# A hybrid decoder step on one core: the down product of the ConvFFN computed as seven block products

## The chip, the cores and the metric

The kernel runs on one core of one Trainium2 chip. The metric is the device time of one execution, in microseconds. The core has five engines that run their own instruction queues in order: TensorE (PE, with its weight loads shown as PEld), VectorE (DVE), ScalarE (ACT), GpSimd (POOL) and SyncE (SP, which here only issues DMAs). They wait for one another by semaphores.

## The reference

One layer of a decoder for a prompt of 1024 tokens and 8 sequences of 8 new tokens, so 1088 columns in all. The part around the change is the gated ConvFFN and the last norm:

```python
    h = rms_norm(x, norm_ffn_g)
    g_full = jnp.concatenate([ffn_past, h @ w_ffn_gate], axis=1)
...
    x = x + (jax.nn.silu(g) * (h @ w_ffn_up)) @ w_ffn_down
...
    y_prompt = rms_norm(xp, norm_final_g)
    y_sample = rms_norm(xs, norm_final_g)
```

Here g is a causal convolution of width 3 over g_full. The model width D is 1024 and the FFN width is 2816. Ahead of it the layer has a convolution head group, a dilated attention with a cache, and an output product with a residual.

## The kernel before

Everything lies with channels on the 128 partitions and the 1088 columns (N) along the free axis. D is 8 tiles of 128 rows (KT), the FFN width 22 tiles, which are worked on in 11 **pairs** (j, j + 11). Each fp32 product is made of three matmuls in the fp32r format: a number is split into a rounded high part (hi, a copy on ACT) and a rest (lo, a subtraction, on DVE for activations and on POOL for weights), and hi·hi, hi·lo and lo·hi are summed in PSUM.

**The gate and up stage.** The normed activations h are cut in 2 by 2 blocks (upper and lower half of D, left and right half of the columns, HN = 544). In place of eight block products, seven are made from sums of blocks. The sums of h are made once and kept in SBUF under the tags b11, t2, b21, t1, t3, b22, t4, eight buffers [128, 544] each. The sums of the weights are made for every pair: `weight_raw` loads them (two raw buffers), `weight_parts` splits them (ACT L902, POOL L903), and `blocks_of_both` makes the sums on DVE (L918 to L921). `block_product` (L840, L842, L843) makes one of the seven: two column halves of 272, for each k three matmuls. Its results lie in `pair` tiles of PSUM (tag g2, four buffers of two banks). `ffn_pair(j)` makes the gate product, the convolution and silu, and the up product; the evictions of the up product are L1099 and L1103, the multiplication by silu(g) is `times` (L1094, L1096), and the two rows u of a pair go whole to DRAM (L1106, L1109), 544 KB each.

**The down stage** has pools of its own. The pairs are taken in groups (GROUPS: 3, 3, 3, 2). For a group, `load_act` reads the rows u (L1133) and splits them (hi on ACT L1135, lo on DVE L1136); `down` runs over the 8 output tiles m, loads and splits the weights (L143, L146, L148), and a plain product (L172 to L174, chunks of 384, 384 and 320 columns) is added to x2[m] (L1158), which was read back from DRAM (L1143). The acts of the next group are loaded in the midst of a group (`between`). The last group of two pairs is run by `last_product` in column chunks (TAIL) with m inside (L1195 to L1197); after each chunk but the first the final norm of the chunk before is made by `last_norm`: `rstd` sums the squares by matmul (L191), makes the root on DVE and ACT (L195 to L206), and spreads it by transposes on PE (L213). The sums of `rstd` have PSUM buffers of their own there (tag r, 2 buffers, beside 5 of tag g).

**Norm before the FFN.** `out_half` makes the output product by column halves; in the second half a hook, `norm_first`, issues the norm of the first half after tile m = 3.

The order of instructions on each engine is set by a scheduler that takes the program's order and its own model of times; a DMA or an instruction can be held behind another by `issue_after`.

Of the kernel before, what the change touches and what calls it, by code (L numbers as in the profile page):

```python
# [24 lines left out]
P = 128  # L25
# [18 lines left out]
GROUPS = ((0, 3), (3, 3), (6, 3), (9, 2))  # L44
TAIL = ((0, 256), (256, 256), (512, 320), (832, 256))
# [12 lines left out]
WR = 2  # L58
# [3 lines left out]
ACTS, XF = 22, 3  # L62
# [15 lines left out]
def trunk_kernel(tc, xT, w_in, w_out, w_gate, w_up, w_down, par, kc, vc, sa, sf, pmask, smask,  # L78
                 yT, kT, vT, ca, cas, cf):
    nc = tc.nc  # L80
    with (
# [817 lines left out]
        def weight_parts(x, new):  # L899
# [5 lines left out]
            return [(hi[:, i:i + 4], lo[:, i:i + 4]) for i in range(0, n // P, 4)]  # L905

        def blocks_of_first(raw):
            return weight_parts(raw[0], [zt("F", "WA", 2, "wa", D, F32R) for _ in range(2)])

        def blocks_of_both(raw):  # L910
            def wide(s):
                return wp.tile([P, D], F32R, tag="W", name=nm(s))

            g, u = raw
            t = wide("w22")
# [6 lines left out]
            s2, s4 = weight_parts(g, [wide("s24") for _ in range(2)])  # L922
            s3, s1 = weight_parts(u, [wide("s31") for _ in range(2)])
# [45 lines left out]
        def norm_first(m, added):  # L969
            if m == 3:  # L970
                r0.append(norm_half(sq0))
# [72 lines left out]
        ud = [dp.tile([P, N], F32, name=f"u{j}") for j in range(NF)]  # L1044
# [9 lines left out]
        def ffn_pair(j):  # L1054
# [46 lines left out]
            def put_u(i, h, ps, x):  # L1101
                o = u[i][:, h * HN:h * HN + HN]
                nc.vector.tensor_add(o, all_of(ps), o if x is None else x)  # L1103
# [12 lines left out]
        zf.__exit__(None, None, None)  # L1116


        zd = zones("D")
        zd.__enter__()  # L1120
        gbank[0], rbank[0] = ("D", "g", 5), ("D", "r", 2)

        def wide(s, dt=F32):
            return zt("D", "X", ACTS, s, N, dt)

        read = []

        def load_act(j0, n):
            act = []
            for i in range(2):  # L1130
                for j in range(j0 + i * HF, j0 + i * HF + n):
                    raw = keep("ur") if j0 == 0 else zt("D", "XR", XF, "ur")
                    read.append(nc.sync.dma_start(raw, ud[j]).ins)  # L1133
                    hi, lo = wide("ah", F32R), wide("al", F32R)
                    nc.scalar.activation(hi, raw, AF.Copy)  # L1135
                    nc.vector.tensor_sub(lo, raw, hi.bitcast(F32))  # L1136
                    act.append((hi, lo))
            return act

        def reload(m):  # L1140
# [180 lines left out]
```

## Time and profile before

| | |
|---|---|
| device time, median of 3 runs | 1427.86 us (1422.45 to 1429.79) |
| profiled execution, device time | 1432.72 us |
| profiled execution, span from first to last instruction | 1430.9 us |
| mean granted TensorE clock | 0.975 of full speed |
| gate and up stage, from first to last matmul of the pairs | about 652 to 1134.7 us of the span |
| down stage, groups 1 to 3 | 1134.7 to 1362.1 us |
| down stage, last group, and last norm | 1362.2 to 1430.9 us |

Times within the profile are microseconds from the start of the span. A row of a group gives busy time, the mean of one instruction and the idle time of the engine just before it, with what ended it. PEclk is the share of full clock granted to TensorE. Matmuls overlap, so the length of one is more than the distance from one to the next.

### The profile page before, as it was taken

The numbers are of one execution on the slowest core, as the hardware profiler recorded it, in microseconds if no ns is written. First come the engines' busy times: TensorE is split into PE (matmuls) and PEld (weight loads), VectorE is DVE, ScalarE is ACT, GpSimd is POOL, SyncE is SP. The second block draws the span as 40 slices with busy tenths as digits, with TensorE's granted clock in tenths as the row PEclk, the third lists the DMA queues.
The fourth block names the chain that finished last, engine by engine and source line by source line (L and its number), as shares of the span: only waits on it lengthen the run. The fifth ranks groups of instructions, "written<-read, shape, count | busy, mean of one in ns | idle before, by whom it ended". The sixth has DMA issues, their size and how long they took to land.

```text
span 1430.9 us, 24745 instructions
## 1 busy us (share of the span) xinstructions
PE 1350.0 (94%) x10011; PEld 1280.5 (89%) x10011; DVE 861.0 (60%) x1649; ACT 514.3 (36%) x982; POOL 431.5 (30%) x303
## 2 busy tenths in 40 slices
PE   6999999999999998976999999999999999999995
PEld 6988889999977777876899999999999889999995
DVE  7398595566574665679756566655656642423146
ACT  5312211457565564345333323333332321212033
POOL 3221111110000115231454445545445211224124
PEclk9999999999999998987999999999999999999998
DMA  7246676746699887340022122122212571414003
GB/s 271 54 139 245 226 255 206 206 141 179 180 276 226 243 228 225 112 162 8 30 91 91 65 87 91 52 70 91 91 62 91 167 291 45 139 48 131 11 9 118
DMA packets 84882, 195.16 MB, mean 136 GB/s; under 512 B 12576, under 2 KB 46752, under 8 KB 84768
## 3 DMA queue, kind: packets, MB, share of 16 engines
q1 hardware_dynamic: 84768, 193.57, 42.8%
q8 instruction: 79, 1.29, 0.4%
q14 instruction: 35, 0.29, 0.1%
HBM read 145.03 MB, written 48.52 MB: 135 GB/s over the span
## 4 chain that ended last, share of the span: by engine, by line
PE 76%; DVE 12%; DMA 6%; issue 2%; POOL 1%; ACT 1%; SPq 1%; POOLq 0%; ACTq 0%; DVEq 0%
PE g L174 9%; PE g L172 9%; PE g L173 9%; PE py L840 4%; PE py L842 4%; PE py L843 4%; DVE cacc L333 4%; PE o L666 3%; PE s L581 3%; PE pz L843 3%; PE pz L842 3%; PE pz L840 3%; PE px L843 3%; PE px L840 3%; PE px L842 3%; PE t L649 3%
## 5 line engine op out<-in xcount | busy, mean ns | idle before, releaser
L148 POOL TENSOR_TENSOR wl<-wr,wh 128x768 fp32r<-128x768 f32 (+2 forms) x61 | 117.1, 1921 | 464.7 <-PE g L174 391.8
L172 PE MATMUL g<-xh,wh 128*128 128x384 f32 (+1 forms) x472 | 158.6, 336 | 0.0
L173 PE MATMUL g<-xl,wh 128*128 128x384 f32 (+1 forms) x472 | 157.4, 333 | 0.0
L174 PE MATMUL g<-xh,wl 128*128 128x384 f32 (+1 forms) x472 | 157.2, 333 | 0.0
L172 PE MATMUL g<-ah,wh 128*128 128x384 f32 (+1 forms) x432 | 141.6, 333 | 5.0 <-ACT ah L1135 3.3
L173 PE MATMUL g<-al,wh 128*128 128x384 f32 (+1 forms) x432 | 143.0, 331 | 1.7 <-DVE al L1136 1.7
L174 PE MATMUL g<-ah,wl 128*128 128x384 f32 (+1 forms) x432 | 142.7, 331 | 0.7 <-POOL wl L148 0.7
L146 ACT ACTIVATE wh<-wr 128x768 fp32r<-128x768 f32 (+2 forms) x62 | 52.0, 838 | 241.0 <-PE g L174 177.5
L903 POOL TENSOR_TENSOR s<-wr,s 128x1024 fp32r<-128x1024 f32 x44 | 107.5, 2444 | 89.7 <-ACT s L902 47.9
L1158 DVE TENSOR_TENSOR x<-g,x 128x384 f32<-128x384 f32 (+1 forms) x72 | 38.0, 534 | 137.4 <-PE g L174 137.2
L622 ACT ACTIVATE y<-y,m 128x128 f32<-128x128 f32 (+1 forms) x192 | 88.4, 463 | 32.9 <-DVE m L610 32.9
L174 PEld LDWEIGHTS g<-xh,wl 128*128 128x128 f32 x472 | 90.0, 191 | 2.3 <-issue 2.1
L585 DVE CUSTOM_DVE_ANT_0 y<-s,pmk 128x128 f32<-128x128 f32 (+1 forms) x192 | 63.9, 378 | 45.8 <-PE s L581 36.9
L172 PEld LDWEIGHTS g<-xh,wh 128*128 128x128 f32 x472 | 90.1, 191 | 1.4 <-issue 1.2
L173 PEld LDWEIGHTS g<-xl,wh 128*128 128x128 f32 x472 | 90.0, 191 | 1.1 <-issue 1.0
L172 PEld LDWEIGHTS g<-ah,wh 128*128 128x128 f32 x432 | 82.0, 191 | 5.9 <-ACT ah L1135 3.6
L173 PEld LDWEIGHTS g<-al,wh 128*128 128x128 f32 x432 | 81.9, 190 | 2.0 <-DVE al L1136 2.0
L174 PEld LDWEIGHTS g<-ah,wl 128*128 128x128 f32 x432 | 81.8, 189 | 1.0 <-POOL wl L148 1.0
L333 DVE SCALAR_TENSOR_TENSOR cacc<-gp,prm,cacc 128x1024 f32<-128x1024 f32 x60 | 80.1, 1335 | 0.1
L1087 DVE SCALAR_TENSOR_TENSOR fc<-gb,prm,fc 128x1104 f32<-128x1104 f32 x44 | 79.0, 1813 | 2.0 <-ACT fc L1085 1.2
L903 POOL TENSOR_TENSOR wa<-wr,wa 128x1024 fp32r<-128x1024 f32 (+1 forms) x23 | 56.3, 2448 | 76.3 <-ACT wa L902 76.3
L381 DVE TENSOR_TENSOR qkv<-g,rb 128x384 f32<-128x384 f32 (+1 forms) x53 | 41.2, 777 | 46.0 <-PE g L174 45.9
(307 smaller groups left out, 4118.1 us busy)
## 6 DMA issues: line engine op xcount, KB each, us to landing
cr<-in_kc SPq DMA_DIRECT2D x24, 768.0 KB, 8.8
cr<-in_vc SPq DMA_DIRECT2D x24, 768.0 KB, 7.7
kk<-dk SPq DMA_DIRECT2D x48, 256.0 KB, 7.3
u<-u SPq DMA_DIRECT2D x22, 544.0 KB, 3.0
ur<-u SPq DMA_DIRECT2D x22, 544.0 KB, 4.8
wr<-in_w_in SPq DMA_DIRECT2D x22, 512.0 KB, 4.9
wr<-in_w_gate SPq DMA_DIRECT2D x22, 512.0 KB, 3.3
wr<-in_w_up SPq DMA_DIRECT2D x22, 512.0 KB, 4.5
```

Source lines behind the costliest of these rows:

```text
L148: lo_eng.tensor_sub(lo, raw, hi.bitcast(F32))
L172: nc.tensor.matmul(ps[c], whi[:, k, :], xh[:, t0:t0 + n], start=(k == 0), stop=False)
L173: nc.tensor.matmul(ps[c], whi[:, k, :], xl[:, t0:t0 + n], start=False, stop=False)
L174: nc.tensor.matmul(ps[c], wlo[:, k, :], xh[:, t0:t0 + n], start=False, stop=(k == nk - 1))
L333: eng.scalar_tensor_tensor(acc[:, :S], gp[:, j:j + S], col(w0 + j), acc[:, :S], op0=ALU.mult, op1=ALU.add)
L585: nc.vector.tensor_tensor_reduce(out=y[:, o:o + n], in0=ps[:, o:o + n], in1=mask, op0=ALU.add, op1=ALU.min, scale=1.0, scalar=3e38, accum_ ...
L622: nc.scalar.activation(y, y, AF.Exp, bias=m[:, 4 * g + i:4 * g + i + 1], scale=-1.0, accum_out=den[:, g, 2 * hd + u, i:i + 1])
L840: nc.tensor.matmul(ps, whi[:, k, :], xh[:, t], start=(start and k == 0), stop=False, skip_group_check=True)
L842: nc.tensor.matmul(ps, whi[:, k, :], xl[:, t], start=False, stop=False, skip_group_check=True)
L843: nc.tensor.matmul(ps, wlo[:, k, :], xh[:, t], start=False, stop=(k == nk - 1), skip_group_check=True)
L903: nc.gpsimd.tensor_sub(lo, x, hi.bitcast(F32))
L1087: nc.vector.scalar_tensor_tensor(c[:, :W], gb[i][:, t:t + W], col(C_FW + 3 * f + t), c[:, :W], op0=ALU.mult, op1=ALU.add)
```

## The change

Nine of the eleven pairs (three groups of three) of the down product are now made by the same seven block products. The two halves of the contraction are rows j and j + 11, the two halves of the output are tiles m and m + 4, and the two halves of the columns are as before. So a group has four units (m, m + 4), a unit seven block products of 18 matmuls with 272 columns, 12 units in all.

The block sums of u are made in `ffn_pair` for the nine pairs, by four subtractions of [128, 544] on DVE (L1124 to L1130), and stored as seven blocks of 272 KB in place of two rows of 544 KB. `load_block` reads a block back into the slot for its low part, makes the high part from it on ACT (L1148) and subtracts on DVE (L1149), 21 blocks for a group. They lie in the slots of the block sums of h, six of eight buffers; the other two hold accumulators: a unit has three results beside its four output blocks (`extra`, e1, e6, e7), which are added in with five additions in the last group (L1204). Evictions are L1179 (DVE) and, for the first group's extra results, L1183 (ACT). The weights of a unit go through `weight_parts` and `blocks_of_both` like those of the FFN.

One pool serves both stages. The last two pairs are made as before by `last_product`, now in four chunks of 272 columns, with acts and weights in slots of the shared pool. `rstd` takes its PSUM from the same four `pair` buffers as the products. The norm of the first half (`norm_first`) is issued after m = 5 in place of m = 3.

```diff
@@ -41,8 +41,9 @@
 BIG = 1e30
 LN2 = float(np.log(2.0))
 CHUNKS = ((0, 384), (384, 384), (768, 320))
-GROUPS = ((0, 3), (3, 3), (6, 3), (9, 2))
-TAIL = ((0, 256), (256, 256), (512, 320), (832, 256))
+GROUPS = ((0, 3), (3, 3), (6, 3))
+LAST = 9
+TAIL = ((0, 272), (272, 272), (544, 272), (816, 272))
...
@@ -896,22 +896,25 @@
                     nc.sync.dma_start(raw[-1], w[i])
             return raw
 
-        def weight_parts(x, new):
+        def weight_parts(x, new, parts=1):
             n = x.shape[-1]
             hi, lo = new
             nc.scalar.activation(hi, x, AF.Copy)
             nc.gpsimd.tensor_sub(lo, x, hi.bitcast(F32))
             hi, lo = [t.rearrange("p (k c) -> p k c", c=P) for t in (hi, lo)]
-            return [(hi[:, i:i + 4], lo[:, i:i + 4]) for i in range(0, n // P, 4)]
+            k = n // P // parts
+            return [(hi[:, i * k:i * k + k], lo[:, i * k:i * k + k]) for i in range(parts)]
...
@@ -967,7 +970,7 @@
         r0 = []
 
         def norm_first(m, added):
-            if m == 3:
+            if m == 5:
                 r0.append(norm_half(sq0))
 
@@ -1041,7 +1044,9 @@
             block_product(z, a22, blocks["t4"], False)
             put(1, 0, z, None)
 
-        ud = [dp.tile([P, N], F32, name=f"u{j}") for j in range(NF)]
+
+        ud = {j: dp.tile([P, N], F32, name=f"u{j}") for i in range(LAST, HF) for j in (i, i + HF)}
+        bd = [{tag: dp.tile([P, HN], F32, name=f"u{tag}{j}") for tag in BTAGS} for j in range(LAST)]
         M = S - HN
         W = GW - 2
 
@@ -1103,98 +1108,153 @@
                 nc.vector.tensor_add(o, all_of(ps), o if x is None else x)
                 if (i, h) == (0, 1):
                     times(0, HN, N)
-                    nc.sync.dma_start(ud[j], u[0])
                 elif x is None:
                     times(1, 0, N)
-                    nc.sync.dma_start(ud[j + HF], u[1])
+                else:
+                    return
+                if j >= LAST:
+                    nc.sync.dma_start(ud[j + i * HF], u[i])
+                    return
+                (x11, x12), (x21, x22) = halves(u[0]), halves(u[1])
+                if i == 0:
+                    nc.sync.dma_start(bd[j]["b11"], x11)
+                    return
+                nc.sync.dma_start(bd[j]["b21"], x21)
+                nc.sync.dma_start(bd[j]["b22"], x22)
+                nc.vector.tensor_sub(x11, x12, x11)
+                nc.sync.dma_start(bd[j]["t1"], x11)
+                nc.vector.tensor_sub(x12, x22, x12)
+                nc.sync.dma_start(bd[j]["t3"], x12)
+                nc.vector.tensor_sub(x22, x22, x11)
+                nc.sync.dma_start(bd[j]["t2"], x22)
+                nc.vector.tensor_sub(x21, x21, x22)
+                nc.sync.dma_start(bd[j]["t4"], x21)
 
             products(weight_blocks(w_up, j) if j else first_up_a + blocks_of_both(first_up), u11, put_u)
 
         for j in range(HF):
             ffn_pair(j)
         nc.sync.dma_start(cf, cfo.rearrange("p j c -> p (j c)"))
...
+
+
+
+        loads = []
+
+        def load_block(tag, j):
+
+            hi, lo = slot(tag, "uh"), slot(tag, "ul")
+            raw = lo.bitcast(F32)
+            loads.append(nc.sync.dma_start(raw, bd[j][tag]).ins)
+            nc.scalar.activation(hi, raw, AF.Copy)
+            nc.vector.tensor_sub(lo, raw, hi.bitcast(F32))
+            return hi, lo
 
         def rows(m, j0, n):
 
             return w_down[m].rearrange("p (i c) -> p i c", i=2)[:, :, j0 * P:(j0 + n) * P]
 
...
+        def down_raw(m, j0, n):
+            raw = []
+            for i in (m, m + 4):
+                t = wp.tile([P, D], F32, tag="WR", name=nm("wr"), bufs=WR)[:, :2 * n * P]
+                nc.sync.dma_start(t.rearrange("p (i c) -> p i c", i=2), rows(i, j0, n))
+                raw.append(t)
+            return raw
+
+        extra = {}
+
+        def down_unit(m, j0, n, ub, first, last):
+            raw = down_raw(m, j0, n)
+            a11, a12, a22, s1, s2, s3, s4 = blocks_of_first(raw) + blocks_of_both(raw)
+            if first:
+                for i in (m, m + 4):
+                    x2[i] = (keep if i in (0, 4, 1, 5, 2) else spare)("x2")
+                    with tc.issue_after(loads[3 * n - 1]):
+                        nc.sync.dma_start(x2[i], x2d[i])
+                extra[m] = [slot(BTAGS[1 + (3 * m + i) // 2], "ex", F32) for i in range(3)]
+            e1, e6, e7 = extra[m]
+            (c11, c12), (c21, c22) = halves(x2[m]), halves(x2[m + 4])
+
+            def add(o, ps):
+                nc.vector.tensor_add(o, all_of(ps), o)
+
+            def put(o, ps):
                 if first:
-                    reload(m)
-
...
+                    nc.scalar.activation(o, all_of(ps), AF.Copy)
+                else:
+                    add(o, ps)
+
+            x, y, z = pair("px"), pair("py"), pair("pz")
+            block_product(x, a11, ub["b11"], True)
+            put(e1, x)
+            block_product(y, s2, ub["t2"], True)
+            put(e6, y)
+            block_product(x, a12, ub["b21"], False)
+            add(c11, x)
+            block_product(y, s1, ub["t1"], False)
+            add(c22, y)
+            block_product(z, s3, ub["t3"], True)
+            put(e7, z)
+            block_product(y, s4, ub["b22"], False)
+            add(c12, y)
+            block_product(z, a22, ub["t4"], False)
+            add(c21, z)
+            if last:
+                for o, e in ((c12, e1), (e6, e1), (e7, e1), (c21, e6), (c22, e7)):
+                    nc.vector.tensor_add(o, o, e)
+
+        for q, (j0, n) in enumerate(GROUPS):
+            ub = {tag: [load_block(tag, j) for j in range(j0, j0 + n)] for tag in BTAGS}
+            for m in range(4):
+                down_unit(m, j0, n, ub, q == 0, q == len(GROUPS) - 1)
+
+
+        nl = HF - LAST
+        act = []
+        for i, j in enumerate(j for j0 in (LAST, LAST + HF) for j in range(j0, j0 + nl)):
+            tag = ("b11", "b11", "t2", "b21")[i]
+            act.append([])
+            for h in range(2):
+                hi, lo = slot(tag, "ah"), slot(tag, "al")
+                raw = lo.bitcast(F32)
+                nc.sync.dma_start(raw, ud[j][:, h * HN:h * HN + HN])
+                nc.scalar.activation(hi, raw, AF.Copy)
+                nc.vector.tensor_sub(lo, raw, hi.bitcast(F32))
+                act[-1].append((hi, lo))
+        nj = len(act)
         w = []
-
...
+        for m in range(KT):
+            if m % 2 == 0:
                 raw = wp.tile([P, D], F32, tag="WR", name=nm("wr"), bufs=WR)
...
+            r = raw[:, m % 2 * 512:m % 2 * 512 + 512]
+            nc.sync.dma_start(r.rearrange("p (i c) -> p i c", i=2), rows(m, LAST, nl))
+            if m < 2:
+                t = zt("F", "WA", 2, "wl", D, F32R)
+            elif m < KT - 1:
+                t = wp.tile([P, D], F32R, tag="W", name=nm("wl"))
+            if m < KT - 1:
+                hi, lo = t[:, :512], t[:, 512:]
+            else:
+                hi, lo = slot("t2", "wh", w=512), slot("t2", "wl", w=512)
+            nc.scalar.activation(hi, r, AF.Copy)
+            nc.gpsimd.tensor_sub(lo, r, hi.bitcast(F32))
+            w.append([t.rearrange("p (k c) -> p k c", c=P) for t in (hi, lo)])
+
+
+        def wide(s):
+            return slot(("t1", "t3", "b22", "t4")[cnt[0] % 4], s, F32)
 
         def last_product(t0, n):
             acc = [None, None]
+            h, t = divmod(t0, HN)
             for m in range(KT):
-                ps = bank(*gbank[0])
+                ps = pair()
...
-        zd.__exit__(None, None, None)
+        zf.__exit__(None, None, None)
         zr.__exit__(None, None, None)
```

Three places show how the instructions now stand. Numbers behind an underscore tell tiles of one name apart.

The first is ScalarE at the turn from one group of pairs to the next. Before, the last copies of the second group's acts (ah) and the weights (wh) of the tiles m:

```order
L146 ACTIVATE wh_12605<-wr_12603 128x768
L146 ACTIVATE wh_12671<-wr_12669 128x768
L1135 ACTIVATE ah_12191<-ur_12189 128x1088
L1135 ACTIVATE ah_12737<-ur_12735 128x1088
L146 ACTIVATE wh_12773<-wr_12771 128x768
L1135 ACTIVATE ah_12743<-ur_12741 128x1088
```

Now, with uh the high part of a block of u for the second group and s_1878 the high part of the weight sum for the first unit of that group (product with t2):

```order
L1148 ACTIVATE uh_12954<-ul_12955 128x544
L1148 ACTIVATE uh_12964<-ul_12965 128x544
L1148 ACTIVATE uh_12959<-ul_12960 128x544
L1148 ACTIVATE uh_12969<-ul_12970 128x544
L1148 ACTIVATE uh_12974<-ul_12975 128x544
L902 ACTIVATE s_1878_12994<-wr_12979 128x768
L902 ACTIVATE s_1880_12998<-wr_12981 128x768
L902 ACTIVATE wa_13142<-wr_13138 128x768
```

The weight parts stood between the acts, ahead of part of them; now the sums of the unit's weights stand behind the last block of the group (uh_12964, uh_12969 and uh_12974 are the blocks with tag t4). TensorE takes the products of that unit in this order, where px is the product with b21 and py_13003 the one with t2:

```order
L840 MATMUL px_13002<-uh_12914,wa_12983 128x272
L842 MATMUL px_13002<-ul_12915,wa_12983 128x272
L843 MATMUL px_13002<-uh_12914,wa_12984 128x272
L840 MATMUL py_13003<-uh_12889,s_1878_12994 128x272
L842 MATMUL py_13003<-ul_12890,s_1878_12994 128x272
L840 MATMUL pz_13004<-uh_12934,s_1880_12998 128x272
L842 MATMUL pz_13004<-ul_12935,s_1880_12998 128x272
L843 MATMUL py_13003<-uh_12889,s_1879_12995 128x272
```

The eighteen matmuls with b21 stand between the last product of the old group (with the old t4) and the first that reads s_1878.

The second place is TensorE in the last product, at the first norm of a chunk. Before, the sums (L191) and, 34 rows later, the transposes (L213):

```order
L1197 MATMUL g_13999<-ah_13319,wl_13348 128x256
L191 MATMUL r_14017<-ones,sq_13761 128x1 x2
L1195 MATMUL g_14055<-ah_13301,wh_13326 128x320
L1196 MATMUL g_14055<-al_13302,wh_13326 128x320
```

```order
L1197 MATMUL g_14087<-ah_13313,wl_13334 128x320
L213 MATMUL r_14031<-ident,rr_14023 128x128 x2
L1195 MATMUL g_14087<-ah_13319,wh_13333 128x320
```

Now:

```order
L1257 MATMUL g_14705<-ah_14406,wl_14450 128x272
L191 MATMUL g_2072_14723<-ones,sq_14467 128x1 x2
L191 MATMUL g_2072_14723<-ones,sq_14467 16x1
L213 MATMUL g_2077_14739<-ident,rr_14731 128x128 x2
L213 MATMUL g_2077_14739<-ident,rr_14731 128x16
L1255 MATMUL g_14764<-ah_14381,wl_14418 128x272
```

Matmuls of the next chunk stood between the sums and the transposes; now nothing does. The same holds for the second norm (42 rows between before, none now). For the third nothing stood between in either kernel.

The third place is VectorE at the end of a pair in the gate and up stage; u are the two rows of the pair, gb is the next pair's gate product, py and pz its results in PSUM. Before:

```order
L1103 TENSOR_TENSOR u_9151<-py_9204,ta_9201 128x544
L1094 TENSOR_TENSOR u_9151<-u_9151,fc_9139 128x480
L1096 TENSOR_TENSOR u_9151<-u_9151,fc_9139 128x64
L1103 TENSOR_TENSOR u_9152<-pz_9205,u_9152 128x544
L1094 TENSOR_TENSOR u_9152<-u_9152,fc_9146 128x1024
L1073 TENSOR_TENSOR gb_9363<-py_9419,ta_9416 128x544
```

Now:

```order
L1108 TENSOR_TENSOR u_10122<-py_10175,ta_10172 128x544
L1099 TENSOR_TENSOR u_10122<-u_10122,fc_10110 128x480
L1101 TENSOR_TENSOR u_10122<-u_10122,fc_10110 128x64
L1124 TENSOR_TENSOR u_10122<-u_10122 128x544
L1108 TENSOR_TENSOR u_10123<-pz_10176,u_10123 128x544
L1099 TENSOR_TENSOR u_10123<-u_10123,fc_10117 128x1024
L1126 TENSOR_TENSOR u_10122<-u_10123,u_10122 128x544
L1128 TENSOR_TENSOR u_10123<-u_10123,u_10122 128x544
L1078 TENSOR_TENSOR gb_10343<-py_10399,ta_10396 128x544
L1130 TENSOR_TENSOR u_10123<-u_10123 128x544
```

Three of the four subtractions stand ahead of the eviction of the next gate product (L1073 before, L1078 now); the fourth follows it.

More of the change, by code (lines that the diff above doesn't have):

```diff
@@ L1115, in trunk_kernel @@
         nc.sync.dma_start(cf, cfo.rearrange("p j c -> p (j c)"))
[L1116 to L1138, printed above, removed]
@@ L1145, in rows @@
         def rows(m, j0, n):
             return w_down[m].rearrange("p (i c) -> p i c", i=2)[:, :, j0 * P:(j0 + n) * P]
-        def down(j0, n, act, first, between):
-            for m in range(KT):
-                if m == 2:
-                    between()
-                w = load_w(rows(m, j0, n), 2 * n, nc.gpsimd)
-                if first:
-                    reload(m)
-                def ev(ps, t0, n, x=x2[m]):
-                    nc.vector.tensor_add(x[:, t0:t0 + n], ps[:, :n], x[:, t0:t0 + n])
-                gemm(w, act, 2 * n, ev)
+        def down_raw(m, j0, n):
[5 more added lines that the diff above has]
+            return raw
```

44 lines of the change are left out of this document (11 added, 33 removed).

## The prediction

> **What bounds the kernel now.** I read the page's busy table and the chain of waits first, then tables by stage, then PE's gaps.
>
> ```profile
> PE 1350.0 (94%) x10011; PEld 1280.5 (89%) x10011; DVE 861.0 (60%) x1649; ACT 514.3 (36%) x982; POOL 431.5 (30%) x303
> PE 76%; DVE 12%; DMA 6%; issue 2%; POOL 1%; ACT 1%; SPq 1%; POOLq 0%; ACTq 0%; DVEq 0%
> ```
>
> TensorE is busy for 94% of the span and holds 76% of the chain that ends last. So a microsecond of matmuls saved counts in full, and a gap on PE costs in full, as long as PE has no other gap to lose it in. Busy time by stage (columns: window, length, then busy and count for PE, PEld, DVE, ACT, POOL; PEclk; DMA share; GB/s):
>
> ```profile
> 800.00:900.00 100.00, 100.00 (x802) 100.00 (x801) 60.51 (x68) 30.32 (x34) 49.15 (x38) 1.00 0.26 87
> 1310.00:1362.00 52.00, 52.00 (x314) 52.00 (x313) 9.16 (x17) 3.40 (x4) 8.89 (x5) 1.00 0.11 31
> 1134.70:1362.40 227.70, 220.27 (x1300) 218.80 (x1299) 73.94 (x96) 44.87 (x47) 52.53 (x27) 0.99 0.35 117
> ```
>
> The gate and up stage and the end of group 3 run without a gap: 100/802 = 0.1247 us for a matmul of 272 columns, and 52/314 = 0.1656 us for the down product's mix (mean 362.7 columns). Per column that is 0.458 and 0.457 ns: a matmul has next to no fixed cost here, and columns are what counts. The whole of groups 1 to 3 takes 227.7 us for 1296 matmuls, which at full pace are 1296 x 0.1656 = 214.6 us: 13.1 us are lost. PE's gaps there:
>
> ```profile
> 1135.86 0.76 PE L172 MATMUL g<-ah,wh 128*128 128x320 f32 x3 [0.60 <-DVE u L1103]
> 1138.32 0.45 PE L173 MATMUL g<-al,wh 128*128 128x384 f32 x1 [1.70 <-DVE al L1136]
> 1151.25 1.91 PE L172 MATMUL g<-ah,wh 128*128 128x384 f32 x5 [3.29 <-ACT ah L1135]
> 1307.18 0.44 PE L172 MATMUL g<-ah,wh 128*128 128x384 f32 x1 [1.15 <-ACT wh L146]
> 1309.14 0.44 PE L174 MATMUL g<-ah,wl 128*128 128x384 f32 x1 [0.70 <-POOL wl L148]
> ```
>
> They sum to 7.4 us. The third brings a second loss, seen in windows of 2 us; the first row stands for comparison:
>
> ```profile
> 1138.00:1140.00 2.00, 1.68 (x10) 1.68 (x11) 2.00 (x3) 0.00 (x0) 0.00 (x0) 1.00 0.96 345
> ...
> 1150.00:1152.00 2.00, 0.75 (x2) 0.75 (x3) 0.77 (x1) 1.69 (x2) 0.00 (x0) 0.65 1.01 418
> 1152.00:1154.00 2.00, 2.00 (x8) 2.00 (x8) 1.96 (x3) 2.00 (x3) 0.00 (x0) 0.50 1.02 420
> 1156.00:1158.00 2.00, 2.00 (x9) 2.00 (x9) 0.26 (x1) 0.00 (x0) 0.00 (x0) 0.64 1.03 422
> ```
>
> After an idle time of 3.29 us the granted clock is 0.50 until about 1157.4 (0.64 over the last window), 6.2 us of work at half pace: 3.1 us lost. I call this the **clock penalty** and charge it to gaps of 3 us or more. After the gap of 1.70 us (first row) the clock stayed at full. The last 2.6 us of the 13.1 are spread in pieces too small to name.
>
> **Part 1, the matmuls.** 1296 matmuls of 362.7 columns become 12 x 126 = 1512 of 272: 1512 x 0.1247 = 188.5 us in place of 214.6: **-26.1**. All the losses of the old stage go with its code: **-13.1**. What the new stage loses in their place follows.
>
> **Part 2, entry into the down product.** The first unit needs 21 blocks (5.7 MB) in the slots that hold the block sums of h. A slot comes free when the last FFN product with its tag ends, for t4 at the very end; and DVE has the last pair's products and 21 low parts to make.
>
> ```profile
> ur<-u SPq DMA_DIRECT2D x22, 544.0 KB, 4.8
> 1135.84 1.22 DVE L1094 TENSOR_TENSOR u<-u,fc 128x1024 f32<-128x1024 f32 x1
> L883 DVE TENSOR_TENSOR t4l<-x,t4h 128x544 fp32r<-128x544 f32 x4 | 2.7, 716 | 0.0
> ```
>
> 21 x 0.72 = 15 us of low parts and, as I count its rows, about as much again of evictions, products and weight sums stand against the unit's 7 x 18 x 0.1247 = 15.7 us and the 18 us of the six FFN products (24 matmuls each) that follow when the first slots come free. VectorE has no slack there, but six tags of seven can be loaded ahead, which the old stage, with six rows of 4.8 us each to load and x2 to read back, could not; so it should be no worse than the old entry (0.60 + 1.70 + 3.29 + 3.1 = 8.7). Bounds 4 (two short waits) and 14 (a longer one and the penalty); I take **+8**, next to the old entry.
>
> **Part 3, the two turns between groups.** A group fills the slots, so a block can be loaded only after the old group's last product with it. On ACT the weight sums of the new unit (s_1878) stand behind all 21 block copies, the last three of which have the tag t4. PE gets to s_1878 only 18 matmuls, 2.2 us, after the old t4 product. From that product's end: load, copies, the high part of the sum; its low part on POOL is needed by the third matmul.
>
> ```profile
> x2d<-x SPq DMA_DIRECT2D x16, 272.0 KB, 2.0
> mx<-mixed SPq DMA_DIRECT2D x4, 272.0 KB, 4.6
> L882 ACT ACTIVATE t4h<-x 128x544 fp32r<-128x544 f32 x4 | 2.6, 657 | 1.3 <-DVE x L1000 1.2
> L146 ACT ACTIVATE wh<-wr 128x768 fp32r<-128x768 f32 x24 | 20.3, 847 | 125.3 <-PE g L174 104.9 <-DMA wr<-in_w_down 9.4 <-PE py L842 6.2
> L148 POOL TENSOR_TENSOR wl<-wr,wh 128x768 fp32r<-128x768 f32 x24 | 46.6, 1943 | 160.0 <-PE g L174 144.8 <-ACT wh L146 15.2
> L1103 DVE TENSOR_TENSOR u<-pz,u 128x544 f32<-128x544 f32 x11 | 7.8, 712 | 0.4 <-PE pz L843 0.4
> ```
>
> Lower end: 2.0 (a 272 KB store, the faster row) + 2 x 0.66 + 0.85 + 1.94 = 6.1, minus the 2.5 us that PE has work = 3.6 us of idle PE. With the load row of the same size: 4.6 + 3 x 0.66 + 0.85 + 1.94 - 2.5 = 6.9. VectorE gives a second chain: it has 17 low parts and 5 evictions ahead of the last weight sum, 22 x 0.72 = 15.8 us from about 6 us after the old b11 product ended; the old t4 product ends 15.7 us after that, so the sum is ready 6.1 + 0.6 later, and 6.7 + 0.85 + 1.94 - 2.5 = 7.0, or 10 where POOL's work slows four or five of the low parts to twice their time. Two chains meet at **7**, which I take. The clock penalty follows: 7 + 3 = 10 a turn (bounds 3.6 and 13), two turns **+20**. What is late next is the product with s_1880, whose parts follow on ACT and POOL by 0.85 and 1.94 us, within a product at half pace (4.5 us): nothing more.
>
> The Trainium skill (page "TensorE: Matmul & The Clock Gate", Part 1) puts the drop at an idle window of about 3.4 us and the recovery at about 3.4 us of sustained work. The drop agrees with the row at 1151.25; the recovery took 6.2 us there, so the row decides. By the page's figure an estimate of the penalty would be 1.7 us and the sum some 4 us lower.
>
> **Part 4, inside the units.** A unit has seven evictions (7 x 0.72) and four weight sums, 7 to 8 us of DVE in 15.7: covered. In the last group five additions of about 0.7 us each come on top and stand before the next unit's sums; the last product's acts and weights wait for slots too. Bounds 0 and 8, **+4**.
>
> **Part 5, the sums of u in the gate and up stage.** Four subtractions more for each of nine pairs. Where they fall:
>
> ```profile
> 882.51 2.41 DVE L1094 TENSOR_TENSOR u<-u,fc 128x480 f32<-128x480 f32 x1
> 885.72 2.68 DVE L1094 TENSOR_TENSOR u<-u,fc 128x1024 f32<-128x1024 f32 x1
> 890.45 0.72 DVE L1073 TENSOR_TENSOR gb<-py,ta 128x544 f32<-128x544 f32 x1 [2.05 <-PE py L843]
> 884.87 2.45 POOL L903 TENSOR_TENSOR s<-wr,s 128x1024 fp32r<-128x1024 f32 x1 [0.47 <-PE pz L843]
> 893.56 0.29 PE L840 MATMUL py<-t1h,s 128*128 128x272 f32 x1
> ```
>
> Before the eviction at 890.45 DVE idles 2.05 us, and PE needs it at 893.56, after 891.17: 2.4 us more. Three subtractions stand ahead of it: 2.2 us at 0.72, up to 4.3 where POOL's subtraction doubles them as it doubled the 1.22 us product to 2.68; one waits for a store of its operand (2.0 us or more). So 0 to 1.1 us a pair; nine pairs, bounds 0 and 10, **+5**. The gaps are too short for a clock penalty. The stores grow from 2 x 544 to 7 x 272 KB a pair, at a DMA share of 0.26 in that window: hidden behind products of 21 us a pass.
>
> **Part 6, norms.** In the last product the transposes now follow the sums at once.
>
> ```profile
> 1385.29 0.50 PE L191 MATMUL r<-ones,sq 128*128 128x1 f32 x4
> 1390.57 0.38 PE L213 MATMUL r<-ident,rr 128*128 128x128 f32 x2
> 1385.83 0.16 DVE L195 TENSOR_SCALAR rv<-r 128x2 f32<-128x2 f32 x1
> 1388.58 0.16 DVE L206 SCALAR_TENSOR_TENSOR rr<-rt,rr 128x2 f32<-128x2 f32 x1
> 1400.63 0.15 DVE L195 TENSOR_SCALAR rv<-r 128x2 f32<-128x2 f32 x1
> 1402.72 0.15 DVE L206 SCALAR_TENSOR_TENSOR rr<-rt,rr 128x2 f32<-128x2 f32 x1
> ```
>
> The roots took from 1385.3 to 1388.7 and from about 1400.3 to 1402.9, covered by matmuls. Without cover PE idles 3.3 and 2.4 us, and the first, as long as the one at 1151, brings a penalty of 3; the second may: bounds 5 and 11, **+9**. The earlier norm shows the same form:
>
> ```profile
> 626.25 1.18 PE L191 MATMUL g<-ones,sq 128*128 128x1 f32 x10 [1.73 <-DVE sq L955]
> 633.24 1.33 PE L213 MATMUL g<-ident,rr 128*128 128x128 f32 x5 [5.81 <-DVE rv L193]
> ```
>
> Two tiles later the first wait (1.73) should vanish, while the 5.81 and its penalty stay, with less work behind it: -3 to +2, **-0.5**. Four equal chunks end with 272 columns in place of 256: about 0, at most +-1.
>
> **The sum.** -26.1 - 13.1 + 8 + 20 + 4 + 5 + 9 - 0.5 = +6.3 us, from the profiled execution's 1432.7 (span 1430.9) to 1439. That execution lies 4.9 above the median of the three runs, 1427.9; the forecast on that scale is **1434**. The saved columns count in full, and the waits at the turns and the norms take them back.
>
> **Rivals.**
> *The waits stay at their lower ends* (the other side: faster than before). Blocks land in 2 us, and the gaps stay too short for the clock: turns 3.6 without penalty (7 for both), entry 4, units 1, FFN 0, last product 5.5, together 17.5 - 0.5 - 39.2 = -22, which is 1406; with one term half way up it is **1411**. For it: the old entry moved 420 GB/s (row 1152), at which three blocks take 2 us, and the other tags' blocks land before, so that only t4 is left at the turn. Against it: every term at its best, and s_1878 behind the t4 copies is a chain in the order itself, which no load speed removes.
> *Turns at their upper end.* VectorE is the engine that is late: low parts slowed by POOL as at 885.72 run to 1.4 us, 17 of them against the 18 us until PE needs the sums. It decides once more than about four of them are slowed; each turn then costs 13 (+6 for both), the entry 14 (+6), the FFN 10 (+5): **1451**. For it: DVE was 60% busy in the FFN window already, and L1094 shows the slowing; against it: POOL has only four weight subtractions a unit.
> *Each matmul costs something fixed.* 216 more matmuls would then give part of the gain back. A line through the two paces above leaves 0.002 us a matmul, 0.4 us in all. The Trainium skill (page "TensorE: Matmul & The Clock Gate", section "Back-to-back issue gap") gives sustained paces of 81 ns at N = 128 and 131 ns at N = 512; a straight line between them, an estimate, makes 100 ns at 272 and about 111 at 362, so the new matmuls would take 151 us against 144. The rows rule that line out; a loss of all 26 us would mean **1460**.
>
> **How the numbers follow.** Forecast (1424 to 1446) 0.52, lower ends 0.22, upper ends 0.23, fixed cost 0.03. A measurement of this kernel tells about 0.5%, 7.1 us, from no change. The forecast's own range is 0.23 slower, 0.25 same, 0.04 faster, since +6.3 lies next to the bound; the lower ends are faster but for 0.01, the upper ends slower. Together faster 0.25, same 0.26, slower 0.49. The range, 1410 to 1455, reaches the middle of the lower case and past that of the upper one, and leaves about 2 in 10 outside.
>
> **What would show it.** Right: PE idle of 4 to 9 us at both turns, released by s (ACT or POOL), with PEclk near 0.5 behind it; L213 in the last product waiting 2 to 4 us for DVE rr, twice; FFN window still near 0.1247 a matmul, short waits for DVE gb; 1512 matmuls in about 188 us of work. Wrong: turns under 3 us, a pace above 0.13, or PE waiting for loads inside the units.

## The result, and the profile after

| | before | changed |
|---|---|---|
| device time, median | 1428.82 us (4 runs) | 1478.15 us (4 runs, 1475.99 to 1497.2) |
| ratio | | 1.038, 95% interval 1.029 to 1.047 |
| span of the profiled execution | 1430.9 us | 1477.6 us |
| start of the gate and up stage | 652.2 | 652.0 |
| its last matmul | 1134.6 | 1180.0 |
| last product's first matmul | 1362.2 | 1395.0 |
| last product to the end | 68.7 us | 82.6 us |

The kernel became 49 us slower, where +6 was forecast. The table already says where: the start of the gate and up stage is unmoved, its end comes 45 us later, and the down groups between take less than before. The last row is 14 us longer, but half of that is no loss: 56 matmuls of the last units (7 us of work) now stand behind the last product's first matmul, as the scheduler mixes the two. One execution among the experiments below, of the kernel with three edits, took 2617.36 us at full granted clock; nothing on record says why, and the ratios leave it out. The page of the changed kernel, busy time and the chain that ended last:

```profile
PE 1351.3 (91%) x10236; PEld 1274.6 (86%) x10236; DVE 990.0 (67%) x1805; ACT 558.6 (38%) x1071; POOL 470.1 (32%) x331
PE 66%; DVE 16%; DMA 7%; issue 6%; POOL 2%; ACT 1%; SPq 1%; POOLq 0%; DVEq 0%; ACTq 0%
```

PE's busy time is what it was (1350.0), though its work fell by 59,000 columns: part of it ran at half clock, and a busy PE is not a PE at its pace. Its share of the chain fell from 76 to 66%. The group of the page that was not there before, then VectorE's group for the same place (gate and up stage, 700 to 1160 us):

```profile
L840 PE MATMUL py<-t1h,s 128*128 128x272 f32 x176 | 56.1, 319 | 27.0 <-DVE gb L1078 27.0
```

```profile
L1128 DVE TENSOR_TENSOR u<-u,u 128x544 f32<-128x544 f32 x9 | 18.9, 2098 | 27.5 <-DMA ub<-u 27.4
```

PE stood idle 27.0 us for the eviction of the gate product (L1078), and VectorE stood idle 27.5 us ahead of L1128, the subtraction that makes t2, released by a DMA: the store of a block of u. The stage by windows (columns as before):

```profile
652.00:742.00 90.00, 76.38 (x527) 73.11 (x527) 69.48 (x94) 36.05 (x49) 36.74 (x26) 0.91 0.13 46
742.00:1143.00 401.00, 374.86 (x2902) 373.11 (x2901) 267.38 (x283) 119.28 (x128) 180.62 (x139) 0.97 0.25 88
1182.00:1240.00 58.00, 53.26 (x399) 51.55 (x398) 28.07 (x39) 20.41 (x32) 21.00 (x13) 0.97 0.45 151
1240.00:1278.00 38.00, 30.37 (x215) 29.37 (x214) 24.28 (x37) 17.75 (x28) 11.22 (x7) 0.87 0.48 161
1320.00:1358.00 38.00, 30.20 (x214) 28.88 (x215) 31.94 (x46) 16.46 (x25) 11.74 (x7) 0.91 0.48 148
1395.00:1460.00 65.00, 60.26 (x458) 59.11 (x457) 39.32 (x79) 25.05 (x54) 25.89 (x27) 0.95 0.20 65
```

At 0.1247 us a matmul, 2902 take 361.9 us; 401 passed, so 39 us were lost from 742 to 1143, where before lost 1.9 (3134 matmuls from 742 to 1134.7). The two turns between groups (1240 to 1278, 1320 to 1358) lost 11.2 and 11.3, the last product 7.9 us. The first row holds 5 us more than before, which ran 565 matmuls from 652.2 to 742: after the first pair PE waited 1.3 and 1.9 us for weight parts whose load stood behind the pair's stores. That one was not tried alone.

**One pair from near.** PE, VectorE, GpSimd and the DMA queue around one of the eight stalls, in four answers of the timeline:

```profile
1055.84 0.39 PE L840 MATMUL py<-t1h,s 128*128 128x272 f32 x1 [3.22 <-DVE gb L1078]
```

```profile
1043.99 2.81 DVE L1124 TENSOR_TENSOR u<-u 128x544 f32<-128x544 f32 x1
...
1048.73 0.73 DVE L1126 TENSOR_TENSOR u<-u,u 128x544 f32<-128x544 f32 x1
1053.10 2.05 DVE L1128 TENSOR_TENSOR u<-u,u 128x544 f32<-128x544 f32 x1 [3.65 <-DMA ub<-u]
1055.08 0.71 DVE L1078 TENSOR_TENSOR gb<-py,ta 128x544 f32<-128x544 f32 x1
```

```profile
1052.23 2.34 POOL L903 TENSOR_TENSOR wa<-wr,wa 128x1024 fp32r<-128x1024 f32 x1 [6.02 <-ACT wa L902]
```

```profile
1047.26 0.37 SPq L896 DMA_DIRECT2D wr<-in_w_up  x1
1048.72 0.32 SPq L1122 DMA_DIRECT2D ub<-u  x1
1049.09 0.42 SPq L1123 DMA_DIRECT2D ub<-u  x1
```

L1128 writes t2 over the block that L1123 stores as b22, so it waits until that store has read it. The store is issued at 1049.09, behind a 512 KB load of weights and the store of b21, and lands 4.0 us later. VectorE, done with L1126 at 1049.46, stands still until 1053.10; by then GpSimd has begun its weight subtraction, and L1128 takes 2.05 us in place of 0.72. The gate eviction behind it in VectorE's queue ends at 1055.79, and PE goes on at 1055.84. The clock after it:

```profile
1054.00:1056.00 2.00, 0.16 (x1) 0.16 (x2) 2.00 (x3) 0.00 (x0) 0.57 (x1) 1.00 0.05 20
1056.00:1058.00 2.00, 2.00 (x13) 2.00 (x14) 0.42 (x1) 0.00 (x0) 0.00 (x0) 0.72 0.70 276
1058.00:1060.00 2.00, 2.00 (x11) 2.00 (x11) 0.00 (x0) 0.00 (x0) 0.00 (x0) 0.50 0.01 1
1060.00:1062.00 2.00, 2.00 (x17) 2.00 (x17) 1.28 (x2) 0.63 (x1) 0.68 (x1) 0.93 0.00 0
```

The granted clock is full for the first microsecond, then 0.50 until about 1060.2. Not every stall is followed by this. The eight, with the time at half clock behind each, worked out from windows of 0.5 us:

| stall ends at | 775.5 | 822.5 | 870.9 | 916.6 | 963.5 | 1010.3 | 1055.8 | 1103.1 |
|---|---|---|---|---|---|---|---|---|
| PE idle, us | 3.00 | 3.27 | 3.53 | 3.51 | 3.06 | 3.05 | 3.22 | 3.50 |
| at half clock, us | 3.4 | 5.7 | 0 | 3.4 | 3.4 | 0 | 3.4 | 3.4 |

The waits sum to 26 us, and the half clock, 22.7 us at half pace, to another 11. Together they are the 37 us that this stretch lost beyond the kernel before.

**The turns and the norms** look as drawn. The first turn, on PE, VectorE, ACT and GpSimd:

```profile
1260.03 0.59 PE L840 MATMUL py<-uh,s 128*128 128x272 f32 x1 [5.32 <-ACT s L902]
1263.35 0.59 PE L843 MATMUL py<-uh,s 128*128 128x272 f32 x1 [1.77 <-POOL s L903]
```

```profile
1258.55 0.54 DVE L924 TENSOR_TENSOR wr<-wr 128x384 f32<-128x384 f32 x1
```

```profile
1259.13 1.58 ACT L902 ACTIVATE s<-wr 128x768 fp32r<-128x768 f32 x2 [1.02 <-DVE wr L924]
```

```profile
1260.05 5.03 POOL L903 TENSOR_TENSOR s<-wr,s 128x768 fp32r<-128x768 f32 x2 [12.93 <-ACT s L902]
```

The last weight sum on VectorE (1258.55), its high part on ACT, its low part on GpSimd: PE waits 5.3 and 1.8 us for the two. And the transposes of the last product's norms:

```profile
1429.70 0.91 PE L213 MATMUL g<-ident,rr 128*128 128x128 f32 x3 [2.86 <-DVE rv L193]
...
1447.47 0.59 PE L213 MATMUL g<-ident,rr 128*128 128x128 f32 x3 [1.88 <-DVE rv L193]
```

### The profile page after: what moved, and what is told of

It reads as the page before. It is cut to its first block, busy times and chain, and to the rows that moved or that the text cites. A ratio compares the mean times of both kernels' runs of the same rounds, so it can differ in the third digit from the quotient of the medians.

```text
span 1477.6 us, 25690 instructions
## 1 busy us (share of the span) xinstructions
PE 1351.3 (91%) x10236; PEld 1274.6 (86%) x10236; DVE 990.0 (67%) x1805; ACT 558.6 (38%) x1071; POOL 470.1 (32%) x331
## 4 chain that ended last, share of the span: by engine, by line
PE 66%; DVE 16%; DMA 7%; issue 6%; POOL 2%; ACT 1%; SPq 1%; POOLq 0%; DVEq 0%; ACTq 0%
PE py L840 5%; PE py L843 5%; PE py L842 5%; PE g L172 5%; PE g L174 5%; PE g L173 5%; DVE cacc L333 4%; PE o L666 3%; PE px L840 3%; PE px L843 3%; PE px L842 3%; PE s L581 3%; PE t L649 3%; PE pz L843 3%; PE pz L842 3%
## 5 line engine op out<-in xcount | busy, mean ns | idle before, releaser
L903 POOL TENSOR_TENSOR s<-wr,s 128x1024 fp32r<-128x1024 f32 (+1 forms) x68 | 155.3, 2291 | 164.3 <-ACT s L902 93.0
L148 POOL TENSOR_TENSOR wl<-wr,wh 128x1024 fp32r<-128x1024 f32 (+1 forms) x37 | 70.4, 1903 | 303.6 <-PE g L174 247.7
L172 PE MATMUL g<-xh,wh 128*128 128x384 f32 (+1 forms) x472 | 158.8, 336 | 0.0
L903 POOL TENSOR_TENSOR wa<-wr,wa 128x1024 fp32r<-128x1024 f32 (+2 forms) x35 | 78.9, 2255 | 136.5 <-ACT wa L902 136.5
L902 ACT ACTIVATE s<-wr 128x1024 fp32r<-128x1024 f32 (+1 forms) x68 | 65.3, 980 | 82.5 <-DVE wr L924 70.7
L172 PEld LDWEIGHTS g<-xh,wh 128*128 128x128 f32 x472 | 90.0, 191 | 1.4 <-issue 1.2
L902 ACT ACTIVATE wa<-wr 128x1024 fp32r<-128x1024 f32 (+2 forms) x35 | 33.3, 955 | 129.9 <-DMA wr<-in_w_up 84.1
L840 PE MATMUL py<-t1h,s 128*128 128x272 f32 x176 | 56.1, 319 | 27.0 <-DVE gb L1078 27.0
L903 POOL TENSOR_TENSOR w<-wr,w 128x512 fp32r<-128x512 f32 (+1 forms) x34 | 41.5, 1221 | 115.9 <-ACT w L902 115.1
L840 PE MATMUL py<-uh,s 128*128 128x272 f32 x216 | 64.8, 300 | 10.8 <-ACT s L902 10.7
L146 ACT ACTIVATE wh<-wr 128x1024 fp32r<-128x1024 f32 (+1 forms) x38 | 31.7, 833 | 113.6 <-PE g L174 72.5
L902 ACT ACTIVATE w<-wr 128x512 fp32r<-128x512 f32 (+1 forms) x34 | 20.1, 593 | 128.4 <-PE py L842 118.6
L843 PE MATMUL py<-uh,s 128*128 128x272 f32 x216 | 64.4, 298 | 3.3 <-POOL s L903 3.3
```

What stands on the lines that cost most here:

```text
L148: lo_eng.tensor_sub(lo, raw, hi.bitcast(F32))
L172: nc.tensor.matmul(ps[c], whi[:, k, :], xh[:, t0:t0 + n], start=(k == 0), stop=False)
L840: nc.tensor.matmul(ps, whi[:, k, :], xh[:, t], start=(start and k == 0), stop=False, skip_group_check=True)
L843: nc.tensor.matmul(ps, wlo[:, k, :], xh[:, t], start=False, stop=(k == nk - 1), skip_group_check=True)
L902: nc.scalar.activation(hi, x, AF.Copy)
L903: nc.gpsimd.tensor_sub(lo, x, hi.bitcast(F32))
```

## The experiments

Each starts from the changed kernel unless it says otherwise; line numbers in a profile are those of the kernel that was run. Runs of the kernel before on the same chip gave 1428.65 us beside four of them (t2 over another block, the norms split, the weight sums first, all three) and 1427.62 beside the other three. The changed kernel's ratio has an interval of 1.029 to 1.047, so a gain of 5 to 8 us against it is within the intervals; there the rows of the trace carry the argument.

### t2 over another block

```diff
-                nc.vector.tensor_sub(x22, x22, x11)
-                nc.sync.dma_start(bd[j]["t2"], x22)
-                nc.vector.tensor_sub(x21, x21, x22)
-                nc.sync.dma_start(bd[j]["t4"], x21)
+                nc.vector.tensor_sub(x11, x22, x11)
+                nc.sync.dma_start(bd[j]["t2"], x11)
+
+                def later(after):
+                    with tc.issue_after(after):
+                        nc.vector.tensor_sub(x21, x21, x11)
+                    nc.sync.dma_start(bd[j]["t4"], x21)
+
+                pending.append(later)
```

The pending part is run behind the next pair's gate eviction.

> Against the changed kernel, only the end of a pair in the gate and up stage differs: t2 is written over t1 (stored long before) in place of over the block stored as b22, and t4 is formed behind the eviction of the next gate product. Theory (the stall of 3.0 to 3.5 us a pair is the wait of the t2 subtraction for the store of b22): the eight waits of PE for the gate eviction fall below 0.5 us each, TensorE stays at full clock there, and with 26 us of waits and 13 us of half clock gone the time is 1437 (1432 to 1445). Rival (VectorE is late by the work of the subtractions and by GpSimd slowing them, three of which still stand ahead of the eviction): 1.3 us or more stay at each pair, and the time is 1455 or more.

Measured: 1439.65 us, ratio 1.0081 (1.0048 to 1.0113). The stage by a window, and VectorE at the same place of a pair:

```profile
742.00:1130.00 388.00, 387.95 (x3103) 387.73 (x3102) 273.20 (x302) 131.71 (x144) 194.83 (x148) 1.00 0.30 101
```

```profile
1021.90 0.73 DVE L1130 TENSOR_TENSOR u<-u,u 128x544 f32<-128x544 f32 x1
1022.55 0.72 DVE L1132 TENSOR_TENSOR u<-u,u 128x544 f32<-128x544 f32 x1
1023.18 0.72 DVE L1080 TENSOR_TENSOR gb<-py,ta 128x544 f32<-128x544 f32 x1
```

3103 matmuls in 388 us: the pace of the kernel before, with no stall and full clock, though three subtractions still stand ahead of the eviction. 38.5 of the 49 us were the wait for one store in each pair, with the half clock behind it, and the rival (VectorE's work) is out. The waits of 1.4 and 1.9 us after the first pair are still there.

### The load behind the stores

```diff
-                with tc.issue_after(last_load):
+                with tc.issue_after(stored[0] if stored and w is w_up else last_load):
                     nc.sync.dma_start(raw[-1], w[i])
```

Here stored[0] is the store of b22 of the pair before; t2 is written over that block as in the changed kernel.

> The changed kernel with one thing moved on the DMA queue: the first load of the next up weights (512 KB) is issued behind the stores of b21, b22 and t3 in place of ahead of b21. The order on VectorE stays. If the store of b22 lands late because it shares the DMA engines with that load, it lands about 2 us after its issue in place of 4, the wait for the gate eviction falls from 3.3 to 1.5 us or less, and with the half clock the time falls by 15 to 30 us, to 1455. If a store's landing takes that long by itself, the waits stay above 2.5 us and the time within 6 us of 1478.

Measured: 1472.65 us, ratio 1.031 (1.0266 to 1.0355). VectorE and PE in one pair:

```profile
1043.54 0.72 DVE L1130 TENSOR_TENSOR u<-u,u 128x544 f32<-128x544 f32 x1 [2.51 <-DMA ub<-u]
1044.18 0.72 DVE L1080 TENSOR_TENSOR gb<-py,ta 128x544 f32<-128x544 f32 x1
```

```profile
1044.95 0.39 PE L840 MATMUL py<-t1h,s 128*128 128x272 f32 x1 [0.75 <-DVE gb L1080]
...
1050.15 0.39 PE L843 MATMUL px<-b11h,wa 128*128 128x272 f32 x1 [1.67 <-POOL wa L905]
```

The mechanism is as thought, and the gain is not. The store of b22, issued at 1040.67, now lands 2.9 us later in place of 4.0, the subtraction runs in 0.72 us since GpSimd hasn't begun, and PE's wait for the eviction falls to 0.35 to 0.8 us in seven pairs of eight (2.3 in one). But the weights are late by the same move: PE waits up to 1.9 us, and in some pairs 0.5 more, for their parts at the up product. One wait took the other's place, and of the 15 to 30 us expected 5.5 came by the medians (inside the 6 us that the rival allowed, though the waits did not stay as it said); in the trace the stage is 5.8 us shorter (522.2 us from its first to its last matmul, 528.0 in the changed kernel).

### The norms split

```diff
+            def hook(m):
+                if i and m == 3:
+                    spread.append(rstd(sums[i - 1], D, wide, TAIL[i - 1][1], True))
+                if i and m == 6:
+                    last_norm(sums[i - 1], *TAIL[i - 1], spread[0])
```

`rstd` is cut in two: sums and roots at m = 3 of the next chunk, transposes at m = 6.

> Against the changed kernel, only the last product differs: the sums of a chunk's norm are issued before tile 3 of the next chunk and the transposes before tile 6, so that 36 matmuls (4.5 us) stand between. Theory (the gaps at the transposes and the clock behind them are paid in full): the waits of 2.86 and 1.88 us and the third of 1.81 go, with the half clock behind the first; the time falls by 6 to 11 us, to 1470. Rival (the last norm's end is set by VectorE and the output, so that PE's gaps are hidden): less than 2 us are gained.

Measured: 1470.69 us, 7.5 us under the changed kernel; the ratio to the kernel before is 1.0293 (1.0258 to 1.0328). The last product:

```profile
1392.00:1452.00 60.00, 58.92 (x468) 57.95 (x466) 43.15 (x87) 26.22 (x57) 29.56 (x31) 1.00 0.23 77
```

468 matmuls take 58.4 of 60 us and the clock is full. In the changed kernel 7.9 us of the stretch from 1395 to 1460 were lost. From the last product's first matmul to the end it is 74.7 us here and 82.6 there: the gaps at the transposes were paid in full, as the theory has it.

### The weight sums first

```diff
+                if after and tag in ("t3", "b22", "t4"):
+                    order.enter_context(tc.issue_after(after[0]))
+                    order.enter_context(tc.issue_after(after[2]))
...
+            if q:
+                ahead = down_weights(0, j0, n)
+                after = list(formed)
```

after[0] is the last weight sum on VectorE, after[2] the high part of s24 on ACT.

> Against the changed kernel, only the turns between groups differ: the weights of a group's first unit come ahead of its blocks in the program, and the copies and low parts of the blocks t3, b22 and t4 are held behind the weight sum s24. Theory (the turns wait because s24 stands behind the block copies and low parts): the idle time before the product with t2 falls from 5.3 and 5.4 us to under 2.5 and the half clock mostly goes; the time falls by 8 to 16 us, to about 1466. Rival (the blocks themselves are late, loads and low parts): the same time is lost at the products with t3, b22 or t4 instead, and the gain is under 4 us.

Measured: 1471.05 us, 7.1 us less than the changed kernel; ratio to the kernel before 1.0286 (1.0246 to 1.0326). PE at the second turn:

```profile
1322.89 0.39 PE L840 MATMUL py<-uh,s 128*128 128x272 f32 x1 [1.60 <-ACT s L904]
1324.79 0.39 PE L843 MATMUL py<-uh,s 128*128 128x272 f32 x1 [1.38 <-POOL s L905]
...
1332.45 0.59 PE L842 MATMUL pz<-ul,s 128*128 128x272 f32 x1 [2.87 <-DVE ul L1155]
```

The wait for s24 fell from 5.4 to 1.6 us (at the first turn from 5.3 to 2.1), and a new one of 2.9 us for the low part of a later block came (VectorE, ul). The gain lies between the 8 to 16 us of the theory and the 4 of its rival, and both hold in part: the order was worth about 7 us, and behind it VectorE is late with the blocks.

### All three, and t1 held as well

The three are t2 over another block, the norms split, and the weight sums first.

> All three edits together. If the three losses are separate and all on TensorE's path, the gains add up: 1478 - 40 - 8 - 12 = 1418 (1410 to 1428), below the kernel before. If VectorE is the real bound, what is gained in one place is lost in another, and the time stays above 1435.

Measured: 1428.68 us, ratio 0.9990 (0.9969 to 1.0011), neither under 1428 nor above 1435. From the changed kernel that is -49.5, against the single gains of 38.5 + 7.5 + 7.1 = 53.1: nearly a sum. The forecast of 1418 had taken 12 for the turns.

The next kernel adds t1 to the blocks whose low parts are held behind the last weight sum:

```diff
-                if after and tag in ("t3", "b22", "t4"):
-                    order.enter_context(tc.issue_after(after[0]))
+                if after and tag in ("t1", "t3", "b22", "t4"):
+                    order.enter_context(tc.issue_after(after[0]))
+                if after and tag in ("t3", "b22", "t4"):
                     order.enter_context(tc.issue_after(after[2]))
```

> All three edits, and at the turns the low parts of t1 also held behind the last weight sum. If VectorE's low parts ahead of the sum are what is left of the turns (2.1 and 1.4 us, 1.6 and 1.4 us, 2.1 us of waits and the half clock behind them), about 2 us less stand ahead of it at each turn and the time falls by 4 to 8 us, to 1422. If GpSimd's 1.9 us and the old group's slots set the turn, nothing changes (within 2 us of 1428.7).

Measured: 1426.19 us, ratio 0.9988 (0.9964 to 1.0011). PE at its first turn, and the window:

```profile
1215.49 0.39 PE L846 MATMUL py<-uh,s 128*128 128x272 f32 x1 [1.42 <-POOL s L908]
...
1220.90 0.39 PE L845 MATMUL pz<-ul,s 128*128 128x272 f32 x1 [1.89 <-DVE ul L1168]
1223.79 0.59 PE L843 MATMUL py<-uh,s 128*128 128x272 f32 x1 [2.24 <-DVE ex L1201]
```

```profile
1200.00:1236.00 36.00, 29.96 (x215) 28.88 (x215) 28.55 (x37) 17.86 (x28) 11.73 (x7) 0.91 0.50 166
```

The wait for the high part of s24 is gone, and waits for blocks and evictions on VectorE came in its place: 215 matmuls take 26.8 of 36 us, so this turn still loses 9 us. VectorE is busy for 28.6 of the 36. By the medians the gain is 2.5 us where 4 to 8 were expected, but the runs of the kernel before beside it were 1.0 us faster too, and the ratio hardly moved (0.9990 to 0.9988): no gain is shown. Neither of these two versions is told from the kernel before.

### The first norm at m = 3 again

> The changed kernel with the first norm issued after m = 3 again. If the place of this norm is worth little (the prediction took -0.5, bounds -3 to 2), the first product of the gate and up stage starts within 2 us of 652.0, where both the kernel before (652.2) and the changed one (652.0) start it. If the later norm was worth something, it starts 3 us or more later.

Measured in one execution: 1473.52 us, the first product at 647.6. By the letter that is earlier than both answers, but the stages before it had themselves run some 4 us faster. From the last wide matmul ahead of the output product's block stage (L172 with mh) to that product it is 51.2 us here, 51.6 in the changed kernel, 51.5 to 53.1 in the six others with m = 5, and 49.1 in the kernel before. So the later norm gains nothing; whether it costs 1 us can't be told.

## Why the prediction was wrong, point by point

**The sign was the likeliest one, the size was wrong by 44 us, and one step, Part 5, holds most of it.** Part 5 said of the three subtractions ahead of the gate eviction: "one waits for a store of its operand (2.0 us or more). So 0 to 1.1 us a pair", and "The gaps are too short for a clock penalty." The place was right (PE waits there, for that eviction); the term was mis-sized. It should have been worked out as a time: the store cannot be issued before the last multiplication of u has ended, at 1048.7, and it goes behind a 512 KB load and another store. It landed 4.0 us after its issue, which with GpSimd's slowing of the subtraction made 3.0 to 3.5 us a pair for eight pairs, and with the half clock 37 us above the kernel before in that stage in place of 5. The price of 2.0 us was the median of 16 other stores of that size, and I let it stand beside the subtractions' time, as if it ran from their start. Put behind one another, the same figures (4.3 + 2.0, against 2.05 + 2.4 of slack) give 1.9 us a pair and not 1.1. The gaps were not too short for the clock either: it fell after six of the eight. The first experiment shows it: with the store no longer waited for, 38.5 us are gone, and 1439.65 lies 5.6 above the forecast, about what the stretch with the first pair lost (5 us, in no term); the other terms were off by 1 to 3 us, up and down. So the slowdown that was measured came for the most part from the step that was wrong, not from the turns and norms that were to bring it.

**The matmuls: right.** 272 columns kept the pace of the gate stage (210 matmuls in the 26 us from 1360 to 1386, 0.124 us each); the fixed-cost rival is out, and with it the straight line drawn in the prediction through the sustained paces of the Trainium skill (page "TensorE: Matmul & The Clock Gate", section "Back-to-back issue gap").

**Entry and units: near.** From 1143 to 1240 us 704 matmuls (305 and 399) take 87.8 of 97 us: 9 lost, against +8 for the entry. The rest of the units lost 3, against +4.

**The turns: right in place, mechanism and size.** 11.2 and 11.3 us against 10 each; the waits were 7.1 and 5.9 us, and s24 behind the copies (ACT) and the low parts (VectorE) were the two chains. What I had not seen is that cutting the first leaves the second: the blocks' low parts and evictions keep VectorE busy, and 7 us were to be had by order, not 22.

**The norms: right.** 7.9 us lost in the last product, less 1.2 won in the end after it, against +9; the split gave 7.5 back. The earlier norm gained nothing, against -0.5.

**The rivals.** The lower ends did not come: the turns lost 22.5 us. The upper-end case had VectorE late by its work, with at most 10 us for the gate stage; there it stood idle, for a store. No rival held an in-place write behind a store in flight, and Part 5 had it only as a part of a term of 5, which is why 1478 lay outside the range.

## What to carry to other kernels

When a buffer is stored and then overwritten in place, the overwriting instruction waits for the store to land, and all that stands behind it in its engine's queue waits too: price it from the moment that the data is complete, through every DMA queued ahead, not by the transfer alone. Write such a result over a buffer whose store is already done, or issue it behind the eviction that TensorE waits for; here the first way was worth 38 us for a few lines, and the second was not tried alone. A saving in matmul columns is soon spent if the engines that feed the new form have no time at its turns: here 26 us of columns and 13 us of old losses were paid back at the turns, in the entry and after the first pair, even with the large stall gone and the norms split.

## What the runs showed that was not expected

**A gap's price in clock isn't set by its length.** Of the eight stalls, the longest (3.53 us) and one of 3.05 us cost no clock at all, and the shortest (3.00 us) did. After five, the half clock began 0.3 to 1.5 us behind the restart and lasted 3.4 us, which cost 1.7; after the 3.27 us gap at 822.53, as after the 3.29 us gap at 1151.25 of the kernel before, it stood from the restart on, for 5.7 and 6.2 us. The Trainium skill (page "TensorE: Matmul & The Clock Gate", Part 1) has a free-running window of about 3.4 us for the drop and the recovery. The five stretches of 3.4 us agree with it; that 3.00 us idle brought the drop and 3.53 did not does not follow from an idle window of that length, and no run here shows what decides it. Taking one price (3.1) for all gaps of 3 us or more was too simple.

**The clock fell without a long gap too.** At the first turn of the kernel with t1 held, no gap is over 2.3 us, and the clock was half from about 1221.6 to 1228.4 (0.91 over the window). With the load behind the stores it fell to half for 3.4 us in four of the eight pairs, where no gap is over 1.9 us. That close short gaps add up would fit both; it is not shown.

**A subtraction with both operands in SBUF waits for GpSimd's.** L1128 took 2.05 us beginning 0.9 us into GpSimd's 2.34 us subtraction, 0.72 where GpSimd was idle, and L1124 2.81 us behind one of 2.45. The Trainium skill (page "SBUF — State Buffer", section "SBUF: two separate sides") tells of a port pair that one of the two holds for a whole instruction; both rows agree: L1128 and L1124 each end 0.6 us after GpSimd does.
